# First stage of a streaming encoder step: squares of x moved off GpSimd, an accumulator read earlier, constants loaded later

## The chip, the cores and the metric

The kernel runs on one core of a Trainium2 chip. The time is the device time of one execution in microseconds. Engines are named as the profile names them: PE (TensorE, matmuls), PEld (its weight loads), DVE (VectorE), ACT (ScalarE), POOL (GpSimd) and SP (SyncE, which here only issues transfers). L196 is line 196 of the kernel before.

## The reference

One layer of a hybrid encoder over 256 prompt rows and 64 sample rows, 320 rows together, 2048 wide, all in float32. The stage that matters here is the first norm, the projection behind it, and the two gates:

```
def rmsnorm(x, g):
    y = xf * lax.rsqrt(jnp.mean(xf * xf, axis=-1, keepdims=True) + EPS)
    return (y * g)
...
    p = h @ w_in
    q, k, v, o, gates, u, z = jnp.split(p, SPLIT_IDX, axis=-1)
    gates = gates + b_gate
    ig = gates[..., :N_HEADS_M]
    lf = jax.nn.log_sigmoid(gates[..., N_HEADS_M:])
```

After it come a recurrence over four heads, a spatial gating over 128-row chunks (its weights are `wsp`, its bias `bsp`; `C0` is the carried state of the recurrence), an output projection of 2048 x 2048, and an MLP of 2048 x 8192 x 2048 with a squared ReLU.

## The kernel before

Activations lie transposed: 128 features on the partitions, the 320 rows (`NT`) along the free axis, so x is 16 tiles (`KT`) of 128 x 320. Float32 products are made of split operands: a value is rounded to `hi`, the rest is `lo`, and three matmuls (hi by hi, hi by lo, lo by hi) add up in PSUM. The norm's factor `R1` is a factor per row, so the projection runs on x times g, and R1 is multiplied in when an accumulator is read.

**First stage** (the loop over k, 16 tiles). For tile k, ACT makes `Xh` (L185) and the rounded weights `hi` of the 512 columns of k and the 100 gate columns (L193). DVE makes `Xl` (L194), `lo` (L196) and the low part of 36 gate columns, which it writes into `hi` (L197). POOL squares x (L204) and adds the square to `sacc` (L205). PE does 14 matmuls: four each at L208, L210 and L212 into four accumulators `kacc`, and two (L213, L214) into `gacc`. The raw weights of a tile, `w0raw`, lie in one of 4 buffers; SP issues the load of tile k+4 when tile k has been read. `hi` and `lo` have 5 buffers each.

**Behind it** stand 168 jobs of one form: 48 matmuls (L93, L94, L97) of 320 columns into one accumulator of tag `mm`, of which there are two. `gacc` holds one of these two. The first jobs are z0 to z7. A job's weights come in two halves of 512 KB into the same 4 raw buffers, and each half is split by ACT (L82) and DVE (L83) in program order. The raw buffer is free again when DVE's L83 has read it.

Each engine works in the order in which the program emits its instructions. `split_until(n)` emits the split of halves up to n, and, ahead of it, the loads four halves on. `gates()` is a generator: it sums `sacc` over the partitions with a matmul by ones (L292), makes `R1` (`rsqrt_to`, L120 to L123), and reads `gacc` by a copy on ACT (L295) and an add on DVE (L296); then it scales the four `kacc` and works out the gates, a piece at each call of `run_side()`. In the kernel before, four halves are split before the generator's first piece. `z_evac(c)` reads the accumulator of job z_c, with squares added to `sacc` on POOL; `zt` are the transposes of its result, which stand on PE ahead of the job two on.

`C0`, `wsp` and `bsp` are loaded from ACT's queue right after the first stage's code, and POOL masks `wsp` by four selects.

Of the kernel before, what the change touches and what calls it, by code (L numbers as in the profile page):

```python
# [19 lines left out]
AF = mybir.ActivationFunctionType  # L20
ALU = mybir.AluOpType
# [3 lines left out]
P = 128  # L25
D = 2048
# [3 lines left out]
NT = NP + NS  # L30
# [10 lines left out]
EPS = 1e-6  # L41
# [5 lines left out]
def emit(tc, A):  # L47
    nc = tc.nc
    act, dve, pe, pool, sp = nc.scalar, nc.vector, nc.tensor, nc.gpsimd, nc.sync
# [15 lines left out]
    def sdt(name):  # L65
        return ps.tile([P, 512], F32, tag="sd", name=name, bufs=6)
# [45 lines left out]
    R1 = cp.tile([P, NT], F32, name="R1")  # L112
    R2 = cp.tile([P, NT], F32, name="R2")
    sacc = cp.tile([P, NT], F32, name="sacc")
    sq_last = R2

    def rsqrt_to(out, ss, n, tmp, tag):

        r0, t = tmp(tag + "r"), tmp(tag + "t")
        act.activation(r0, ss, AF.Abs_reciprocal_sqrt, scale=1.0 / n)  # L120
        dve.tensor_tensor(t, r0, r0, ALU.mult)
        dve.scalar_tensor_tensor(t, ss, -0.5 / n, t, ALU.mult, ALU.mult)
        dve.scalar_tensor_tensor(out, t, 1.5, r0, ALU.add, ALU.mult)  # L123
# [4 lines left out]
    def tmp320(name, n=P):  # L128
        t = ap.tile([P, NT], F32, tag="t", name=name, bufs=5)
        return t[:n, :]  # L130
# [14 lines left out]
    def load_x(k0, k1):  # L145
        c = k0 // XC
        sp.dma_start(xraw[c][:, k0 - c * XC:k1 - c * XC, :], A["xg"][:, k0:k1, :])

    def load_w(k):
        w0raw[k] = wp.tile([P, W0], F32, tag="raw", name=f"w0raw{k}", bufs=4)  # L150
        for c0, c1 in W0A if k == 0 else ((0, W0),):
            sp.dma_start(w0raw[k][:, c0:c1], A["w0"][:, k, c0:c1])
# [17 lines left out]
    for c0, n in ((0, 256), (256, 128), (384, 64)):  # L170
        pool.affine_select(MASK[:, c0:c0 + n], MASK[:, c0:c0 + n], [[1, n]], ALU.is_ge, BIG,
                           base=0, channel_multiplier=-1)
# [3 lines left out]
    for k in range(KT):  # L176
        if k == 1:
            load_x(XC, 2 * XC)
        if k == XC:
            load_x(2 * XC, KT)  # L180
        if k + 4 < KT:
            load_w(k + 4)
        xr = xraw[k // XC][:, k % XC, :NT]
        gk = xraw[k // XC][:, k % XC, NT:]
        act.activation(Xh[k][:], xr, AF.Copy, scale=gk)  # L185
        w = w0raw[k]
        hi = wp.tile([P, W0], F32R, tag="hi", name=f"w0hi{k}")
        lo = wp.tile([P, 4 * P], F32R, tag="lo", name=f"w0lo{k}")
        if k == 0:
            for c0, c1 in W0A:  # L190
                dve.tensor_copy(hi[:, c0:c1], w[:, c0:c1])
        else:
            act.copy(hi[:], w[:])  # L193
        dve.scalar_tensor_tensor(Xl[k][:], xr, gk, Xh[k].bitcast(F32)[:], ALU.mult, ALU.subtract)  # L194
        hf = hi.bitcast(F32)
        dve.tensor_tensor(lo[:], w[:, :4 * P], hf[:, :4 * P], ALU.subtract)  # L196
        dve.tensor_tensor(hi[:, 4 * P + 64:], w[:, 4 * P:4 * P + 36], hf[:, 4 * P:4 * P + 36],  # L197
                          ALU.subtract)
        if k == 0:
            pool.tensor_tensor(sacc[:], xr, xr, ALU.mult)  # L200
            pool.tensor_scalar(sacc[:], sacc[:], D * EPS / P, None, ALU.add)
        else:
            sq = tmp320(f"sqx{k}")
            pool.tensor_tensor(sq, xr, xr, ALU.mult)  # L204
            pool.tensor_tensor(sacc[:], sacc[:], sq, ALU.add)  # L205
        first, last = k == 0, k == KT - 1
        for h in range(H):
            pe.matmul(kacc[h][:, :NT], hi[:, h * P:h * P + P], Xh[k][:], start=first, stop=False)  # L208
        for h in range(H):
            pe.matmul(kacc[h][:, :NT], hi[:, h * P:h * P + P], Xl[k][:], start=False, stop=False)  # L210
        for h in range(H):
            pe.matmul(kacc[h][:, :NT], lo[:, h * P:h * P + P], Xh[k][:], start=False, stop=last)  # L212
        pe.matmul(gacc[:100, :NT], hi[:, 4 * P:], Xh[k][:], start=first, stop=False)  # L213
        pe.matmul(gacc[:100, :NT], hi[:, 4 * P:], Xl[k][:], start=False, stop=last)  # L214


    C0 = ap.tile([P, H, VP], F32, name="C0")
    act.dma_start(C0[:], A["c0"])
    wsp = ap.tile([P, 4, P], F32, name="wsp")
    act.dma_start(wsp[:], A["wspT"])  # L220
    bsp = ap.tile([P, 4, P], F32, name="bsp")
    act.dma_start(bsp[:], A["bsp"].partition_broadcast(P))
    for g in range(4):
        pool.affine_select(wsp[:, g, :], wsp[:, g, :], [[1, P]], ALU.is_ge, 0.0,
                           base=0, channel_multiplier=-1)


    qT = [yslot("h", 8 + h, f"qT{h}") for h in range(H)]
# [34 lines left out]
    def later(gen, delay):  # L263
        coros.append([cur[0] + delay, gen])
# [19 lines left out]
    def row(i, name, n=4):  # L284
        return yslot("h" if i < 8 else "l", i % 8, name)[:n, :]
# [4 lines left out]
    def gates():  # L290
        s = sdt("ss1")
        pe.matmul(s[:, :NT], ones[:], sacc[:], start=True, stop=True)  # L292
        rsqrt_to(R1[:], s[:, :NT], D, tmp320, "r1")
        g36, glo = row(0, "g36", 36), row(1, "glo", 36)
        act.copy(glo, gacc[64:100, :NT])  # L295
        dve.tensor_tensor(g36, gacc[:36, :NT], glo, ALU.add)  # L296
        for h in range(H):
            dve.scalar_tensor_tensor(kT[h][:], kacc[h][:, :NT], float(P) ** -0.5, R1[:],
                                     ALU.mult, ALU.mult)
            if h == 1:  # L300
                yield
# [276 lines left out]
    pre = {}  # L578
# [100 lines left out]
    def load_to(n):  # L679
        while loaded[0] < min(n, len(halves)):  # L680
            j, h = halves[loaded[0]]
            j.load(h)
            loaded[0] += 1

    def split_until(n):
        while splitted[0] < min(n, len(halves)):
            load_to(splitted[0] + 4)
            j, h = halves[splitted[0]]
            j.split(h)
            splitted[0] += 1  # L690

    split_until(4)
    later(gates(), 0)
    for i, job in enumerate(jobs[:-1]):
        cur[0] = i
        if i == NA:
# [74 lines left out]
    k = 0  # L771
# [95 lines left out]
```

## Time and profile before

| | |
|---|---|
| median of 3 runs | 1364.63 us (1364.18 to 1366.63) |
| the profiled execution's own time | 1362.95 us |
| its span, first to last instruction | 1361.2 us |
| PE busy in the span | 1348.5 us, 99% |
| DVE, ACT, POOL busy | 688.3, 539.6, 55.4 us |
| moved by the DMA engines | 207.04 MB |

The span is 1.75 us shorter than the execution's time; what lies around it is not in the trace. Matmuls are pipelined and their ends are modelled, so a row of PE is read by the distance from start to start, and not by its duration. A row of DVE, ACT or POOL holds the time in which the instruction stood in the engine, so it can hold time in which it was held up; successive rows of one engine overlap by up to 0.1 us.

### The profile page before, as it was taken

Reading aid. Unit: us, or ns where it says so; the run is one execution under the profiler, and the core shown is the slowest. Engines: PE = TensorE matmul, PEld = TensorE weight load, DVE = VectorE, ACT = ScalarE, POOL = GpSimd, SP = SyncE. Lnnn points to the kernel's source line nnn. Section 1 sums busy time; section 2 is a strip of 40 time slices with the busy share of each in tenths; the row PEclk is TensorE's granted clock in tenths of the full one; section 3 lists DMA queues with packets and bytes.
Section 4 is the critical chain, followed back from the end, with each engine's and each line's share of the span. In section 5 each row is a group of like instructions: output and inputs, shape, how many; then the busy total and the mean of one; then the engine's idle time right before and its main releaser. Section 6 shows DMA issues by size and latency. Waiting matters only on the chain.

```text
span 1361.2 us, 22124 instructions
## 1 busy us (share of the span) xinstructions
PE 1348.5 (99%) x9197; PEld 1339.1 (98%) x9197; DVE 688.3 (51%) x967; ACT 539.6 (40%) x751; POOL 55.4 (4%) x89
## 2 busy tenths in 40 slices
PE   9999999999999999999999999999999999999997
PEld 8899999999999999999999999999999999999997
DVE  8785655565555544443344443444443444444444
ACT  5544465543444434333234433234433233444331
POOL 9410000000000000000000000000000000000000
PEclk9999999999999999999999999999999999999998
DMA  6745433434644444444444454444444444444432
GB/s 217 242 142 176 156 109 132 161 126 161 209 143 154 155 150 146 155 154 144 151 148 147 147 161 146 150 150 145 146 163 145 150 155 140 147 147 156 154 125 78
DMA packets 60023, 207.04 MB, mean 152 GB/s; under 512 B 6592, under 2 KB 9024, under 8 KB 59924
## 3 DMA queue, kind: packets, MB, share of 16 engines
q1 hardware_dynamic: 56932, 199.43, 45.1%
q10 hardware_dynamic: 2960, 6.17, 1.3%
q8 instruction: 72, 1.18, 0.3%
q14 instruction: 27, 0.22, 0.1%
q0 software_dynamic: 32, 0.03, 0.0%
HBM read 201.67 MB, written 3.94 MB: 151 GB/s over the span
## 4 chain that ended last, share of the span: by engine, by line
PE 95%; DVE 2%; issue 1%; DMA 1%; SPq 0%; ACT 0%; DVEq 0%; ACTq 0%
PE acc_f L93 22%; PE acc_f L94 22%; PE acc_f L97 22%; PE acc_out L93 3%; PE acc_out L97 3%; PE acc_out L94 3%; PE acc_u L93 1%; PE acc_v L97 1%; PE acc_o L97 1%; PE acc_v L93 1%; PE acc_o L93 1%; PE acc_u L97 1%; PE acc_o L94 1%; PE acc_v L94 1%; PE acc_u L94 1%; PE acc_z L93 1%
## 5 line engine op out<-in xcount | busy, mean ns | idle before, releaser
L83 DVE TENSOR_TENSOR lo_f<-raw_f,hi_f 128x1024 fp32r<-128x1024 f32 x256 | 306.2, 1222 | 139.2 <-ACT hi_f L82 137.3
L82 ACT CAST hi_f<-raw_f 128x1024 fp32r<-128x1024 f32 x256 | 261.9, 1052 | 236.4 <-PE acc_f L94 236.4
L93 PE MATMUL acc_f<-x2h,hi_f 128*128 128x320 f32 x1024 | 302.6, 309 | 0.0
L94 PE MATMUL acc_f<-x2l,hi_f 128*128 128x320 f32 x1024 | 302.4, 309 | 0.0
L94 PE MATMUL acc_f<-Yl,hi_f 128*128 128x320 f32 x1008 | 297.7, 309 | 0.0
L93 PE MATMUL acc_f<-Yh,hi_f 128*128 128x320 f32 x1008 | 297.6, 309 | 0.0
L93 PEld LDWEIGHTS acc_f<-x2h,hi_f 128*128 128x128 f32 x1024 | 192.3, 188 | 0.1
L94 PEld LDWEIGHTS acc_f<-x2l,hi_f 128*128 128x128 f32 x1024 | 192.3, 188 | 0.1
L93 PEld LDWEIGHTS acc_f<-Yh,hi_f 128*128 128x128 f32 x1008 | 189.3, 188 | 0.0
L94 PEld LDWEIGHTS acc_f<-Yl,hi_f 128*128 128x128 f32 x1008 | 189.3, 188 | 0.0
L97 PE MATMUL acc_f<-x2h,lo_f 128*128 128x320 f32 x1024 | 171.0, 309 | 0.0
L97 PE MATMUL acc_f<-Yh,lo_f 128*128 128x320 f32 x1008 | 168.3, 309 | 0.0
L97 PEld LDWEIGHTS acc_f<-x2h,lo_f 128*128 128x128 f32 x1024 | 155.4, 188 | 0.0
L97 PEld LDWEIGHTS acc_f<-Yh,lo_f 128*128 128x128 f32 x1008 | 153.0, 188 | 0.0
L653 ACT ACTIVATE f<-f 128x320 f32<-128x320 f32 x64 | 30.3, 473 | 262.3 <-DVE f L652 262.3
L659 DVE TENSOR_TENSOR xres<-acc_f,xres 128x320 f32<-128x320 f32 x63 | 31.0, 492 | 142.1 <-PE acc_f L97 142.1
L652 DVE SCALAR_TENSOR_TENSOR f<-acc_f,R 128x320 f32<-128x320 f32 x64 | 31.5, 492 | 136.8 <-PE acc_f L97 136.6
L94 PE MATMUL acc_out<-Yl,hi_out 128*128 128x320 f32 x256 | 75.6, 309 | 0.0
L93 PE MATMUL acc_out<-Yh,hi_out 128*128 128x320 f32 x256 | 75.6, 309 | 0.0
L280 DVE TENSOR_TENSOR Yl<-f,Yh 128x320 fp32r<-128x320 f32 x64 | 31.5, 493 | 66.1 <-ACT Yh L279 66.1
L93 PEld LDWEIGHTS acc_out<-Yh,hi_out 128*128 128x128 f32 x256 | 48.1, 188 | 0.0
L94 PEld LDWEIGHTS acc_out<-Yl,hi_out 128*128 128x128 f32 x256 | 48.0, 188 | 0.0
(333 smaller groups left out, 1667.8 us busy)
## 6 DMA issues: line engine op xcount, KB each, us to landing
raw_f<-w_ff SPq DMA_DIRECT2D x256, 512.0 KB, 3.9
raw_out<-w_out SPq DMA_DIRECT2D x32, 512.0 KB, 5.0
raw_z<-w_z SPq DMA_DIRECT2D x16, 512.0 KB, 5.0
raw_v<-w_v SPq DMA_DIRECT2D x16, 512.0 KB, 5.5
raw_o<-w_o SPq DMA_DIRECT2D x16, 512.0 KB, 5.0
raw_u<-w_u SPq DMA_DIRECT2D x16, 512.0 KB, 4.6
w0raw<-w SPq DMA_DIRECT2D x15, 306.0 KB, 2.9
raw_q<-w_q SPq DMA_DIRECT2D x8, 512.0 KB, 4.3
```

What stands on the lines that cost most here:

```text
L82: act.copy(hi[:], raw[:])
L83: dve.tensor_tensor(lo[:], raw[:], hi.bitcast(F32)[:], ALU.subtract)
L93: pe.matmul(o, self.hi[h][:, k, :], xh, start=(h == 0 and k == 0), stop=False)
L94: pe.matmul(o, self.hi[h][:, k, :], xl, start=False, stop=False)
L97: pe.matmul(o, self.lo[h][:, k, :], xh, start=False, stop=(h == 1 and k == 7))
L280: dve.tensor_tensor(l_[:], src, h_.bitcast(F32)[:], ALU.subtract)
L652: dve.scalar_tensor_tensor(t[:], acc, 0.0, R2[:], ALU.max, ALU.mult)
L653: act.activation(t[:], t[:], AF.Square)
L659: dve.tensor_tensor(xres[m], acc, xres[m], ALU.add)
```

## The change

The squares of x are made on ACT. The first goes straight into `sacc`, and DVE adds the 15 others, the constant included with the first of these. POOL has no arithmetic left in this stage. `gates()` reads `gacc` before it makes `R1`, and yields once after `R1`; the caller emits this first piece after one split half and not after four. `C0`, `wsp` and `bsp` are loaded, and `wsp` is masked, in `load_late()`, which is called ahead of the matmuls of job 3 (z3).

```
         if k == 0:
-            pool.tensor_tensor(sacc[:], xr, xr, ALU.mult)
-            pool.tensor_scalar(sacc[:], sacc[:], D * EPS / P, None, ALU.add)
+            act.activation(sacc[:], xr, AF.Square)
         else:
             sq = tmp320(f"sqx{k}")
-            pool.tensor_tensor(sq, xr, xr, ALU.mult)
-            pool.tensor_tensor(sacc[:], sacc[:], sq, ALU.add)
+            act.activation(sq, xr, AF.Square)
+            if k == 1:
+                dve.scalar_tensor_tensor(sacc[:], sq, D * EPS / P, sacc[:], ALU.add, ALU.add)
+            else:
+                dve.tensor_tensor(sacc[:], sacc[:], sq, ALU.add)
...
+    def load_late():
+        act.dma_start(C0[:], A["c0"])
+        act.dma_start(wsp[:], A["wspT"])
+        act.dma_start(bsp[:], A["bsp"].partition_broadcast(P))
+        for g in range(4):
+            pool.affine_select(wsp[:, g, :], wsp[:, g, :], [[1, P]], ALU.is_ge, 0.0,
+                               base=0, channel_multiplier=-1)
...
         pe.matmul(s[:, :NT], ones[:], sacc[:], start=True, stop=True)
-        rsqrt_to(R1[:], s[:, :NT], D, tmp320, "r1")
         g36, glo = row(0, "g36", 36), row(1, "glo", 36)
         act.copy(glo, gacc[64:100, :NT])
         dve.tensor_tensor(g36, gacc[:36, :NT], glo, ALU.add)
+        rsqrt_to(R1[:], s[:, :NT], D, tmp320, "r1")
+        yield
...
+    pre[3] = load_late
+    split_until(1)
+    gate_chain = gates()
+    next(gate_chain)
     split_until(4)
-    later(gates(), 0)
+    later(gate_chain, 0)
```

DVE at the end of the first stage, before: the last two tiles (xl, lo, the 36 columns), four halves of jobs z0 and z1, the three operations of R1, and the read of the gate accumulator, g.

```order
L194 SCALAR_TENSOR_TENSOR xl_117<-xraw_121,xh_101 128x320
L196 TENSOR_TENSOR w0lo_528<-w0raw_426,w0hi_527 128x512
L197 TENSOR_TENSOR w0hi_527<-w0raw_426,w0hi_527 128x36
L194 SCALAR_TENSOR_TENSOR xl_118<-xraw_121,xh_102 128x320
L196 TENSOR_TENSOR w0lo_552<-w0raw_452,w0hi_551 128x512
L197 TENSOR_TENSOR w0hi_551<-w0raw_452,w0hi_551 128x36
L83 TENSOR_TENSOR lo_z_0_637<-raw_z_0_628,hi_z_0_636 128x1024
L83 TENSOR_TENSOR lo_z_1_643<-raw_z_1_630,hi_z_1_642 128x1024
L83 TENSOR_TENSOR lo_z_0_649<-raw_z_0_632,hi_z_0_648 128x1024
L83 TENSOR_TENSOR lo_z_1_655<-raw_z_1_634,hi_z_1_654 128x1024
L121 TENSOR_TENSOR r1t<-r1r 128x320
L296 TENSOR_TENSOR g_666<-gacc,glo 36x320
...
```

The same place of DVE after the change (its lines have other numbers: the read of `gacc` is L300, the added sums are L207).

```order
L194 SCALAR_TENSOR_TENSOR xl_118<-xraw_121,xh_102 128x320
L196 TENSOR_TENSOR w0lo_551<-w0raw_451,w0hi_550 128x512
L197 TENSOR_TENSOR w0hi_550<-w0raw_451,w0hi_550 128x36
L207 TENSOR_TENSOR sacc<-sacc,sqx_556 128x320
L83 TENSOR_TENSOR lo_z_0_629<-raw_z_0_620,hi_z_0_628 128x1024
L300 TENSOR_TENSOR g_634<-gacc,glo 36x320
L121 TENSOR_TENSOR r1t<-r1r 128x320
L122 SCALAR_TENSOR_TENSOR r1t<-ss_632,r1t 128x320
L123 SCALAR_TENSOR_TENSOR R_81<-r1t,r1r 128x320
L83 TENSOR_TENSOR lo_z_1_647<-raw_z_1_622,hi_z_1_646 128x1024
L83 TENSOR_TENSOR lo_z_0_653<-raw_z_0_624,hi_z_0_652 128x1024
L83 TENSOR_TENSOR lo_z_1_659<-raw_z_1_626,hi_z_1_658 128x1024
```

Each tile has one instruction more on DVE, and the read of `gacc` and the three operations of R1 have moved past three of the four halves.

ACT at the same place, before: the three loads of the constants stand between the last tile and z0.

```order
L185 ACTIVATE xh_102<-xraw_121 128x320
L193 CAST w0hi_551<-w0raw_452 128x612
L218 DMA C_574<-c 128x1032
L220 DMA wsp<-wspT 128x512
L222 DMA bsp<-bsp 128x512
L82 CAST hi_z_0_636<-raw_z_0_628 128x1024
L82 CAST hi_z_1_642<-raw_z_1_630 128x1024
L82 CAST hi_z_0_648<-raw_z_0_632 128x1024
L82 CAST hi_z_1_654<-raw_z_1_634 128x1024
L120 ACTIVATE r1r<-ss_658 128x320
L295 COPY glo<-gacc 36x320
```

And after.

```order
L185 ACTIVATE xh_102<-xraw_121 128x320
L193 CAST w0hi_550<-w0raw_451 128x612
L203 ACTIVATE sqx_556<-xraw_121 128x320
L82 CAST hi_z_0_628<-raw_z_0_620 128x1024
L299 COPY glo<-gacc 36x320
L120 ACTIVATE r1r<-ss_632 128x320
L82 CAST hi_z_1_646<-raw_z_1_622 128x1024
L82 CAST hi_z_0_652<-raw_z_0_624 128x1024
L82 CAST hi_z_1_658<-raw_z_1_626 128x1024
```

No table load was added on ACT, the copy of `gacc` now stands behind one half, and the three loads are gone from here.

POOL after the change, further on: the masks of `wsp` stand between two of the z jobs' additions to `sacc` (before, they stood ahead of all of them).

```order
L394 TENSOR_SCALAR sacc<-sacc 128x320
L397 TENSOR_TENSOR sacc<-sacc,zr_796 128x320
L407 MEMSET z2g 64x1024
L397 TENSOR_TENSOR sacc<-sacc,zr_879 128x320
L228 AFFINE_SELECT wsp<-wsp 128x128
L228 AFFINE_SELECT wsp<-wsp 128x128 x3
L397 TENSOR_TENSOR sacc<-sacc,zr_966 128x320
```

The first of them waits for the load of `wsp`, and the addition for z3 stands behind it. The order of PE's matmuls and of SP's loads is what it was.

## Rows read from the trace of the kernel before

**Rows 1.** Waits of PE, whole span: us in total, times, longest.
```profile
PE acc_z L93 <- DVE g L296: 1.7, 1, 1.7
PE ssf_s L737 <- ACT R L732: 0.7, 1, 0.7
```

**Rows 2.** Waits of PEld, whole span, the two longest.
```profile
PEld kacc L212 <- DVE w0lo L196: 4.6, 15, 0.3
PEld acc_z L93 <- DVE g L296: 2.0, 1, 2.0
```

**Rows 3.** Timeline, DVE, one tile: start, us, line, operation.
```profile
34.30 1.37 DVE L196 TENSOR_TENSOR w0lo<-w0raw,w0hi 128x512 fp32r<-128x512 f32 x1
35.59 0.71 DVE L197 TENSOR_TENSOR w0hi<-w0raw,w0hi 128x36 fp32r<-128x36 f32 x1
36.22 0.54 DVE L194 SCALAR_TENSOR_TENSOR xl<-xraw,xh 128x320 fp32r<-128x320 f32 x1
36.68 1.37 DVE L196 TENSOR_TENSOR w0lo<-w0raw,w0hi 128x512 fp32r<-128x512 f32 x1
```

**Rows 4.** Timeline, POOL, the same tile.
```profile
33.94 1.18 POOL L205 TENSOR_TENSOR sacc<-sacc,sqx 128x320 f32<-128x320 f32 x1
35.08 1.17 POOL L204 TENSOR_TENSOR sqx<-xraw 128x320 f32<-128x320 f32 x1
```

**Rows 5.** Busy time, tile 1 to 15: PE, PEld, DVE, ACT, POOL; clock, DMA share, GB/s.
```profile
9.50:42.87 33.37, 32.76 (x196) 28.52 (x196) 33.37 (x44) 16.05 (x27) 31.67 (x28) 1.00 0.65 206
```

**Rows 6.** Timeline, DVE, first tile and last tile.
```profile
6.38 0.68 DVE L196 TENSOR_TENSOR w0lo<-w0raw,w0hi 128x512 fp32r<-128x512 f32 x1
...
42.74 0.18 DVE L197 TENSOR_TENSOR w0hi<-w0raw,w0hi 128x36 fp32r<-128x36 f32 x1
```

**Rows 7.** Groups by line and shape, DVE and ACT: busy us, mean ns.
```profile
L83 DVE TENSOR_TENSOR lo_z<-raw_z,hi_z 128x1024 fp32r<-128x1024 f32 x16 | 19.0, 1214 | 7.8 <-ACT hi_z L82 7.8
...
L628 DVE TENSOR_TENSOR sacc<-sacc,sq 128x320 f32<-128x320 f32 x27 | 13.2, 489 | 7.0 <-ACT sq L624 7.0
...
L624 ACT ACTIVATE sq<-xres 128x320 f32<-128x320 f32 x29 | 13.5, 464 | 59.0 <-DVE xres L659 59.0
L193 ACT CAST w0hi<-w0raw 128x612 fp32r<-128x612 f32 x15 | 10.6, 707 | 13.3 <-PE gacc L214 5.6 <-DMA w0raw<-w 5.5 <-DVE w0lo L196 2.0
...
L185 ACT ACTIVATE xh<-xraw 128x320 fp32r<-128x320 f32 x16 | 9.0, 560 | 3.7 <-DMA xraw<-xg 3.7
```

**Rows 8.** The chain that ended last, two runs of eight matmuls.
```profile
92.74 1.17 PE acc_z L97 x8
...
96.26 1.17 PE acc_z L97 x8
```

**Rows 9.** Page, DMA issues: KB each, us to landing.
```profile
w0raw<-w SPq DMA_DIRECT2D x15, 306.0 KB, 2.9
```

**Rows 10.** Busy time from 40 to 50 us; the last column is GB/s.
```profile
40.00:50.00 10.00, 9.91 (x65) 9.19 (x64) 6.33 (x8) 4.08 (x4) 6.40 (x22) 1.00 0.86 316
```

**Rows 11.** Timeline, PE: tile 1's first matmuls, and the sum of squares behind tile 15.
```profile
8.12 0.75 PE L208 MATMUL kacc<-xh,w0hi 128*128 128x320 f32 x4
...
43.85 0.70 PE L292 MATMUL ss<-sacc,ones 128*128 128x320 f32 x2
```

**Rows 12.** Timeline, PE, from job z0 to job z1.
```profile
50.26 1.34 PE L97 MATMUL acc_z<-xh,lo_z 128*128 128x320 f32 x8
...
53.56 0.30 PE L94 MATMUL acc_z<-xl,hi_z 128*128 128x320 f32 x1
```

**Rows 13.** The z weights' tile view, its line on transfers.
```profile
DMA to landing us min/median/max: 3.7/5.0/6.6
```

**Rows 14.** DMA issues up to 70 us: the largest constant.
```profile
C<-c ACTq DMA_DIRECT2D x1, 516.0 KB, 5.5
```

**Rows 15.** Timeline, ACT: the casts of job z5's two halves.
```profile
70.31 1.98 ACT L82 CAST hi_z<-raw_z 128x1024 fp32r<-128x1024 f32 x2
```

**Rows 16.** The chain that ended last: PE's transposes ahead of z5.
```profile
82.70 0.33 PE zt L405 x3
```

More of the change, by code (lines that the diff above doesn't have):

```diff
@@ L217, in emit @@
     C0 = ap.tile([P, H, VP], F32, name="C0")
-    act.dma_start(C0[:], A["c0"])
     wsp = ap.tile([P, 4, P], F32, name="wsp")
-    act.dma_start(wsp[:], A["wspT"])
     bsp = ap.tile([P, 4, P], F32, name="bsp")
[L222 to L225, printed above, removed]
+    def load_late():
[5 more added lines that the diff above has]
+                               base=0, channel_multiplier=-1)
     qT = [yslot("h", 8 + h, f"qT{h}") for h in range(H)]
```

## The prediction

> **What bounds the kernel now.** I begin with what PE waits for, since PE fills the span. After the start it waits twice: 1.7 us at the first matmul of job z1, for DVE's read of the gate accumulator, and 0.7 us at the very end [rows 1]. So from z1 on the time is a row of matmuls without a hole, and only what happens before that can change the end. PE's weight loads tell a second thing: in the first stage they wait 15 times, once in each tile from the second on, always for DVE's `lo` [rows 2]. PE looks busy there (32.76 of 33.37 us) because the ends of matmuls are modelled, but DVE is busy for all 33.37 us and POOL for 31.67 [rows 5]. The tile's period is DVE's: from one `lo` to the next, 36.68 - 34.30 = 2.38 us [rows 3].
>
> What fills that period: `lo` for 1.37 us, the 36 gate columns for 0.71, `xl` for 0.54, laid end to end with a small overlap [rows 3]. Two of these are not DVE's own work. The `lo` of the first tile, same shape, took 0.68 us, and the 36 columns of the last tile, when POOL had finished, took 0.18 [rows 6]. In the tile shown, `lo` begins while POOL's sum is running and ends 0.55 us after that sum ends at 33.94 + 1.18 = 35.12; the 36 columns end at 36.30, POOL's square at 36.25 [rows 3, 4]. The two engines hold each other up in turn. The row thus says that of 2.38 us some 1.2 are waiting.
>
> The Trainium skill ("SBUF — State Buffer", Who interferes with whom) has a rule for this: a VectorE instruction with two SBUF inputs and a GpSimd instruction that reads SBUF exclude each other, and the later one waits for the other to end. These rows agree in `lo` and in the 36 columns; `xl`, which has two SBUF inputs as well, stayed at 0.54, so its turn came when POOL was the one to wait. By the rule alone, as by the rows, the waits go when POOL's reads go.
>
> **The squares.** Per tile DVE loses the waits and gains one addition. With durations without POOL: `lo` 0.68, 36 columns 0.18 [rows 6], `xl` 0.54 [rows 3], the sum 0.49, taken from the same addition of the later norms [rows 7]. That makes 1.89 us, or about 1.6 from start to start with the overlaps. ACT has 0.56 + 0.71, and gets a square at 0.46 from the same later norms [rows 7]: 1.73. These stand against PE's own 14 matmuls. A matmul of 320 columns takes (96.26 - 92.74) / 24 = 0.1467 us in the jobs [rows 8], so a tile takes 2.05 us: more than DVE's or ACT's sum even without overlap. So I take PE as the next bound of this stage. The clock was 1.00 of full speed there, which is the 2.4 GHz level [rows 5], and there is nothing above it.
>
> The weights have to keep up. A raw buffer comes back for tile k+4 when tile k has been read; load 2.9 us [rows 9], cast 0.71, `lo` 0.68, 36 columns 0.18 make about 4.5 us for four tiles, 1.1 us each, and even a load twice as long leaves 1.85. The transfers move 206 GB/s in this stage [rows 5]; at 2.05 instead of 2.38 us a tile they need 240, and 316 has been reached in 40 to 50 us [rows 10].
>
> Tile 1's first matmul starts at 8.12 us [rows 11], after a first tile whose few waits are for its own loads, so I leave that start where it is. Fifteen tiles of 14 matmuls then take 30.81 us, and the sum of squares behind them starts at 38.93 instead of 43.85 [rows 11]: **4.92 us earlier**. Bounds: if nothing is gained, 0; if tile 1's start also moved as far forward as its `lo` wait of 0.3 us [rows 2], 5.2.
>
> **The gate accumulator.** z0's last eight matmuls start at 50.26 and advance 1.17 us [rows 12, 8], so the second matmul of z1 could start at 51.58; it starts at 53.56 [rows 12]. That is 1.98 us, the 2.0 us which the weight load waits [rows 2]. After the change the copy and the add stand behind one half only. `gacc` is complete at about 39 us, so it is read by about 40, while z0 occupies PE until 38.93 + 0.30 + 48 x 0.1467 = 46.27. The wait is gone with 6 us to spare: **1.98 us**. What now comes later is the split of z0's second half and of z1: copy, add and the three operations of R1 put it at about 41.5 us on DVE. PE wants z0's second `lo` at 39.23 + 40 x 0.1467 = 45.1, and it is done at 42.7; z1's two halves follow at 43.9 and 45.1, wanted at 48.6 and 52.1. A step further: z2's second half is loaded only when z0's second `lo` has freed its buffer at 42.7. With the median landing of 5.0 us [rows 13], a cast of about 1.0 [rows 15] and a `lo` of 1.21 [rows 7], z0's accumulator is read at 50.6; PE comes to z2 at 53.3. With the slowest landing, 6.6 us, it is 52.2, still in time. I charge nothing, and up to 1 us in the range.
>
> **The constants.** Their loads took about 1 MB (the largest is 516 KB [rows 14]) beside the first loads of z. Nothing in PE waited for those, so taking them away gives nothing. At the new place, ACT issues them after z2's evacuation and before the casts of z5. Those casts stood at 70.31 us and PE came to z5 at 82.70 [rows 15, 16]: a lead of 12 us, against 1.4 us of issuing. In bytes, 1 MB at 316 GB/s [rows 10] is 3.3 us of all transfers, which the lead covers as well. POOL waits for `wsp` there with z3's addition behind it; the sum of these additions is wanted five jobs later. I charge 0, and 3.3 us as the price if the cover fails. POOL's memsets move to the first microseconds, where POOL had its first square; 0 too.
>
> **Sum.** 4.92 + 1.98 = 6.90. The profiled execution took 1362.95 us, so 1356.05 by its own scale, with a span of about 1354.3. That execution was 1.68 us quicker than the median; against the median of 1364.63 the forecast is **1357.7 us**.
>
> **Rivals.**
> 1. DVE stays the bound, and the added sum lengthens it: *slower*. For it speaks that DVE shows no idle time at all in this stage [rows 5], and the change adds work to it. If `lo` and the 36 columns kept their length for another reason than POOL, the period would be 2.38 + 0.49 = 2.87 us, 14 periods 6.9 us longer, less 1.98: 1369.5. It turns slower in total above a period of 2.38 + 1.98 / 14 = 2.52 us. Against it stand the 0.68 and the 0.18 [rows 6]. The Trainium skill ("Perfetto Trace Analysis", Optimizing Scalar/DVE Operations) would give work of a saturated DVE to ScalarE or even GpSimd, which is against these 15 additions; it says in the same place that GpSimd shares a port with DVE, and the rows side with that. Chance 0.04.
> 2. The stage speeds up less: loads, or semaphores between ACT and DVE, hold the tile at about 2.2 us. ACT waited 5.5 us in all for the weights [rows 7]. Then 15 x 0.15 = 2.2 us are lost: 1359.9. Chance 0.08.
> 3. The constants at the fourth job hold up weights: 3.3 us back, 1361.0. The 12 us of lead speak against it. Chance 0.03.
> 4. Only the accumulator's wait goes, because another engine takes over at the old period: 1362.7, no measurable change. Chance 0.03.
>
> **How the numbers follow.** The forecast itself gets 0.82, with 1356.2 to 1359.0 as its own range (1 us of a new wait, and the spread of the runs shown, which is about 1 us to either side). The range 1355.6 to 1360.9 takes in rival 2 and most of rival 3. A change of 0.2%, 2.7 us, is about what can be told from none, so 1361.9 and below counts as faster: the forecast, rivals 2 and 3 make 0.93; rival 4 and a little of the others 0.04 as the same; rival 1 0.03 to 0.04 as slower. I give 0.92, 0.04, 0.04.
>
> **What would show it.** In the profile after: `lo` at about 0.68 us and the 36 columns at 0.2 in every tile; DVE with idle time between tiles; no 0.3 us waits of weight loads for `lo`; the sum-of-squares matmul at about 39 us; no wait of z1 for the gate add; DVE's added sums at 0.49 and ACT's squares at 0.46; the rest of PE without a hole, and the span near 1354.3. Wrong would be: `lo` still above 1 us, ACT waiting for weights in each tile, or a new wait of PE at z2 or between z4 and z6.

## The result and the profile after

The changed kernel took **1358.07 us** (median of 4 runs, 1356.24 to 1358.90), the kernel before beside it 1364.57. The ratio is 0.9948, with a 95% interval of 0.9930 to 0.9965: 6.5 us faster by the medians, 7.1 by the ratio. The profiled execution took 1358.22 us, with a span of 1356.5 us.

PE's waits in the profile after, whole span, to be read beside [rows 1]:

```profile
PE warm L164 <- DVE eps L110: 1.1, 1, 1.1
PE ssf_s L747 <- ACT R L742: 0.6, 1, 0.6
PE kacc L210 <- ACT w0hi L193: 0.5, 1, 0.5
PE kacc L210 <- DVE w0hi L191: 0.2, 1, 0.2
```

The wait of z1 for the gate add is gone. What is left lies in the first 8.3 us and at the very end. One tile on DVE (L207 is the added sum), the counterpart of [rows 3], and the stretch that answers to [rows 5]:

```profile
11.41 0.68 DVE L196 TENSOR_TENSOR w0lo<-w0raw,w0hi 128x512 fp32r<-128x512 f32 x1
12.01 0.19 DVE L197 TENSOR_TENSOR w0hi<-w0raw,w0hi 128x36 fp32r<-128x36 f32 x1
12.12 0.48 DVE L207 TENSOR_TENSOR sacc<-sacc,sqx 128x320 f32<-128x320 f32 x1
12.52 0.55 DVE L194 SCALAR_TENSOR_TENSOR xl<-xraw,xh 128x320 fp32r<-128x320 f32 x1
12.98 0.68 DVE L196 TENSOR_TENSOR w0lo<-w0raw,w0hi 128x512 fp32r<-128x512 f32 x1
```

```profile
10.43:39.18 28.75, 28.75 (x198) 28.75 (x197) 22.45 (x56) 19.31 (x40) 0.00 (x0) 1.00 0.80 266
```

`lo` has fallen from 1.37 to 0.68 us and the 36 columns from 0.71 to 0.19. With one instruction more, DVE needs 12.98 - 11.41 = 1.57 us for a tile and stands idle for 6.3 us of the 28.75. PE's weight loads (the third number) now fill the stretch, where they had been busy for 28.52 of 33.37. PE's timeline, with the places of [rows 11] and [rows 12] (the start of tile 1, the sum of squares, the last matmuls of z0, the second matmul of z1):

```profile
8.28 0.85 PE L210 MATMUL kacc<-xh,w0hi 128*128 128x320 f32 x4 [0.48 <-ACT w0hi L193]
...
39.18 0.70 PE L297 MATMUL ss<-sacc,ones 128*128 128x320 f32 x2
...
45.58 1.34 PE L97 MATMUL acc_z<-xh,lo_z 128*128 128x320 f32 x8
...
46.90 0.31 PE L94 MATMUL acc_z<-xl,hi_z 128*128 128x320 f32 x1
```

The sum of squares starts at 39.18 and not at 43.85, z1's second matmul at 46.90 and not at 53.56: a lead of 6.66 us, against 6.90 forecast. Yet the spans differ by 1361.2 - 1356.5 = 4.7 us only. The other 1.9 us go at the end. These are the last matmuls, 64 columns each, and the sum behind them, first after the change, then before it:

```profile
1341.82 1.06 PE L734 MATMUL acc_s<-Yh,lo_f 128*128 128x64 f32 x8
1342.71 1.47 PE L734 MATMUL acc_s<-Yh,hi_f 128*128 128x64 f32 x8
1343.99 1.89 PE L734 MATMUL acc_s<-Yl,hi_f 128*128 128x64 f32 x8
...
1348.19 0.69 PE L747 MATMUL ssf_s<-R,ones 128*128 128x64 f32 x2 [0.60 <-ACT R L742]
```

```profile
1349.36 1.06 PE L724 MATMUL acc_s<-Yh,hi_f 128*128 128x64 f32 x8
...
1352.90 0.69 PE L737 MATMUL ssf_s<-R,ones 128*128 128x64 f32 x2 [0.70 <-ACT R L732]
```

Up to 1342.71 the changed kernel is 6.65 us ahead. From there to the last sum it takes 5.48 us, where the kernel before took 3.54. The busy times by stretch, after the change, show why (the granted clock stands third from the end):

```profile
1342.50:1343.00 0.50, 0.50 (x7) 0.50 (x6) 0.47 (x2) 0.00 (x0) 0.00 (x0) 1.00 0.00 0
1343.00:1343.50 0.50, 0.50 (x5) 0.50 (x5) 0.47 (x2) 0.00 (x0) 0.00 (x0) 0.70 0.00 0
1343.50:1344.00 0.50, 0.50 (x5) 0.50 (x4) 0.50 (x2) 0.00 (x0) 0.00 (x0) 0.50 0.00 0
```

The clock falls to its lower level, 1.2 GHz, in the middle of the narrow matmuls. In the profile before it fell too, but only when they were over. The profile of e3 below, which has the end of the kernel before, shows the same fall in the middle of them:

```profile
1349.00:1350.00 1.00, 1.00 (x6) 1.00 (x6) 0.97 (x4) 0.00 (x0) 0.00 (x0) 0.50 0.00 0
```

So this is no wait that the change has made. It is a loss that falls on some executions and not on others, of either kernel: the four runs of the changed kernel were 1358.22, 1358.90 and 1357.91 us with a mean clock of 0.995, and 1356.24 us with 0.997.

### The profile page after: what moved, and what is told of

Read it like the earlier page. It is cut to its first block, busy times and chain, and to the rows that moved or that the text cites. A ratio compares the mean times of both kernels' runs of the same rounds, so it can differ in the third digit from the quotient of the medians.

```text
span 1356.5 us, 22119 instructions
## 1 busy us (share of the span) xinstructions
PE 1346.4 (99%) x9197; PEld 1341.5 (99%) x9197; DVE 676.4 (50%) x982; ACT 542.2 (40%) x767; POOL 18.3 (1%) x57
## 4 chain that ended last, share of the span: by engine, by line
PE 99%; DMA 0%; DVE 0%; SPq 0%; ACT 0%; issue 0%; DVEq 0%
PE acc_f L94 22%; PE acc_f L93 22%; PE acc_f L97 22%; PE acc_out L93 3%; PE acc_out L97 3%; PE acc_out L94 3%; PE acc_u L93 1%; PE acc_z L97 1%; PE acc_v L97 1%; PE acc_o L97 1%; PE acc_v L93 1%; PE acc_o L94 1%; PE acc_z L93 1%; PE acc_u L97 1%; PE acc_v L94 1%; PE acc_o L93 1%
```

## The experiments

Theory A is that of the prediction: POOL's reads held DVE, the early read of `gacc` removes the wait of z1, the constants' place is worth nothing, and the parts add up. Theory B is that the wait of z1 was a consequence of the slow stage, and the parts overlap.

### One part at a time

**e1_squares**: the kernel before with the first hunk of the diff alone.

> The kernel before with only the squares of x moved to ACT and DVE; gate accumulator and constants as before. Theory A (the parts add up, as in the prediction's sum): the sum of squares starts at about 39.2 us, z1 still waits about 2 us for the gate add, so 4.7 us faster than before. Theory B (the gate wait was itself caused by late landings of the z weights, which are asked for when first-stage buffers come free): with a faster first stage the landings come earlier too, the wait of z1 shrinks below 0.5 us, so 6 to 6.7 us faster than before. If POOL was not what held DVE up, the stage keeps its length and the time is that of before or up to 7 us more.

Measured: 1357.41 us (5 runs, 1356.04 to 1359.64) against 1364.29, ratio 0.9955 (0.9943 to 0.9968): 6.9 us faster by the medians, 6.1 by the ratio, where the whole change had 6.5 and 7.1: no difference can be told. The profile says the same more sharply. In the profiled execution the clock stayed up to the last matmuls, as in that of the kernel before, and the spans are 1354.2 and 1361.2 us: 7.0 less. The sum of squares starts at 38.79. The gate add, and z0's last matmuls on PE:

```profile
45.17 0.47 DVE L298 TENSOR_TENSOR g<-gacc,glo 36x320 f32<-36x320 f32 x1
...
45.19 1.34 PE L97 MATMUL acc_z<-xh,lo_z 128*128 128x320 f32 x8
```

The add still stands behind four split halves and R1, and is done at 45.64, before z1 is due at 46.36. No wait is left. Theory B.

**e2_gate**: the kernel before with the hunk in `gates()` and the order at the call.

> The kernel before with only the order around the gates changed (one split, then the read of the gate accumulator, then R1, then three splits). First stage as before, sum of squares at 43.85 us. Theory A and B: the 2.0 us wait of z1 is gone, 2.0 us faster than before. Rival: another wait takes its place at z1 (its weights land late beside the constants' loads): less than 1 us faster.

Measured: 1362.26 us (11 runs), ratio 0.9987 (0.9979 to 0.9996): 2.0 us faster by the medians, 1.8 by the ratio (0.5 to 2.9), and z1's wait for the gate add is gone from the profile. The sum of squares is at 44.69 there and not at 43.85 as told: in the first two tiles POOL's reads met other instructions of DVE than in the profile before (the first `lo` took 1.20 us in place of 0.68, an `xl` 1.05 in place of 0.54). Alone, the early read does what the prediction says.

**e3_late**: the kernel before with `load_late()` at job 3.

> The kernel before with only the three constants' loads and the masks moved to job 3. Theory A (constants cost nothing before): no change, gate wait of z1 still 2 us. Theory B (their 1 MB delays the z halves, ACT's casts of four halves, and behind these the copy of the gate accumulator): z1's wait falls from 2.0 to below 0.5 us, 1.5 to 2 us faster than before.

Measured: 1363.03 us (11 runs), 1.3 us less than before, ratio 0.9995 (0.9986 to 1.0004): the interval holds no change as well. The profile tells more. ACT's cast ahead of R1 and z1's first matmul:

```profile
48.15 1.05 ACT L82 CAST hi_z<-raw_z 128x1024 fp32r<-128x1024 f32 x1 [0.90 <-DMA raw_z<-w_z]
...
52.36 0.41 PE L93 MATMUL acc_z<-xh,hi_z 128*128 128x320 f32 x1 [0.57 <-DVE g L298]
```

The fourth half is cast at 48.15 and not at 49.09, the gate add starts at 51.83 and not at 52.78, and z1's wait on PE is 0.57 us, not 1.7. Of these 1.15 us, 0.2 are not the add's: PE came later, with the sum of squares at 44.05. So the constants did delay the z weights and, behind them, the gate add. Theory A's zero for them is wrong in this kernel; by the clock of the runs alone it stays open.

The three parts measured alone make 6.9 + 2.0 + 1.3 = 10.2 us by the medians, together 6.5 (8.6 and 7.1 by the ratios): two of them remove a wait that the first removes as well. The traces show it without the scatter of the runs. From the sum of squares to the second matmul of z1 it is 9.71 us in the kernel before, 7.72 in e1, 7.90 in e2, 8.56 in e3, and 7.72 with all three.

### What POOL did to DVE

**e5_pool_reads** and **e6_pool_writes**: the changed kernel with work on POOL whose result (in R2, overwritten later) nothing uses. The second has `pool.memset(R2[:], 0.0)` twice in place of the two lines.

```diff
+        pool.tensor_tensor(R2[:], xr, xr, ALU.mult)
+        pool.tensor_tensor(R2[:], xr, xr, ALU.mult)
         first, last = k == 0, k == KT - 1
```

> The changed kernel with two multiplications of x by itself on POOL in each tile of the first stage, into a buffer that nothing reads (the work that POOL had, without its results). Theory A (DVE and POOL exclude each other when both read two operands from SBUF): lo goes back above 1 us and the 36 columns above 0.5, the tile's period to 2.4 to 2.8 us, and the time is 5 to 11 us more than that of the changed kernel: 1363 to 1369. Rival (moving the sums' dependence off POOL was what counted, POOL's mere activity costs nothing): 1358, period 2.05.

> The changed kernel with two memsets of 128 x 320 on POOL in each tile of the first stage, into a buffer that nothing reads before it is overwritten. Theory A (it is reads that exclude each other): period 2.05, lo 0.68, time of the changed kernel, 1358. Rival (any SBUF traffic of POOL holds DVE up): lo and the 36 columns longer; whether the time moves depends on whether DVE's tile passes 2.05 us.

Measured: with the reads 1366.03 us (10 runs), 2.4 more than the kernel before beside it (1363.61); with the writes 1357.68 (4 runs). DVE with POOL reading, one tile:

```profile
22.96 1.01 DVE L194 SCALAR_TENSOR_TENSOR xl<-xraw,xh 128x320 fp32r<-128x320 f32 x1
23.89 1.20 DVE L196 TENSOR_TENSOR w0lo<-w0raw,w0hi 128x512 fp32r<-128x512 f32 x1
25.01 0.71 DVE L197 TENSOR_TENSOR w0hi<-w0raw,w0hi 128x36 fp32r<-128x36 f32 x1
...
26.05 1.00 DVE L194 SCALAR_TENSOR_TENSOR xl<-xraw,xh 128x320 fp32r<-128x320 f32 x1
```

The period is 3.09 us, longer than the 2.8 expected at most, since now `xl` is held up too (1.01 in place of 0.54), which before was the one that went first. The time is in the range told all the same, because POOL runs ahead and has done its last read before DVE has done its tiles. DVE and then POOL, at that point:

```profile
36.25 1.20 DVE L196 TENSOR_TENSOR w0lo<-w0raw,w0hi 128x512 fp32r<-128x512 f32 x1
...
38.87 0.68 DVE L196 TENSOR_TENSOR w0lo<-w0raw,w0hi 128x512 fp32r<-128x512 f32 x1
...
40.44 0.68 DVE L196 TENSOR_TENSOR w0lo<-w0raw,w0hi 128x512 fp32r<-128x512 f32 x1
...
36.98 1.05 POOL L209 TENSOR_TENSOR R<-xraw 128x320 f32<-128x320 f32 x1
```

POOL's last read ends at 38.03. The next `lo` is back at 0.68 us and the period at 40.44 - 38.87 = 1.57, within one execution, while POOL goes on with memsets up to 40.6 us. With POOL writing, DVE and then POOL:

```profile
12.58 0.68 DVE L196 TENSOR_TENSOR w0lo<-w0raw,w0hi 128x512 fp32r<-128x512 f32 x1
13.18 0.19 DVE L197 TENSOR_TENSOR w0hi<-w0raw,w0hi 128x36 fp32r<-128x36 f32 x1
...
12.57 0.37 POOL L208 MEMSET R<- 128x320 f32 x1
13.00 0.36 POOL L209 MEMSET R<- 128x320 f32 x1
```

The memsets ran ahead, one after the other up to 17.6 us, some five tiles of DVE; beside them DVE's durations are those without POOL. The Trainium skill ("SBUF — State Buffer", Who interferes with whom) says just this: a VectorE instruction with two SBUF inputs contends with a GpSimd instruction that reads SBUF, and not with one that only writes it. Both runs agree. With e1, which takes POOL's reads away, and e5, which puts them back, the cause of the stage's old period is shown.

### How near DVE is to being the bound

**e7_dve_squares**: the changed kernel with

```diff
-            act.activation(sq, xr, AF.Square)
+            dve.tensor_tensor(sq, xr, xr, ALU.mult)
```

> The changed kernel with the 15 later squares on DVE as well, none on ACT. DVE then has five operations a tile. If durations add up: 0.54 + 0.69 + 0.19 + 0.49 + 0.49 = 2.40 us a tile, DVE the bound, 15 x 0.35 = 5 us slower than the changed kernel: 1363. If what counts is start to start (1.57 us a tile seen in the changed kernel, plus 0.41): 1.98 us, just under PE's 2.05, and the time stays within 0.5 us of 1358.

Measured: 1359.40 us (4 runs, 1356.91 to 1359.72), against 1357.68 of e6 on the same chip (1357.54 to 1359.67). Neither number was met for DVE's tile:

```profile
23.25 0.19 DVE L197 TENSOR_TENSOR w0hi<-w0raw,w0hi 128x36 fp32r<-128x36 f32 x1
23.35 0.49 DVE L203 TENSOR_TENSOR sqx<-xraw 128x320 f32<-128x320 f32 x1
23.87 0.49 DVE L207 TENSOR_TENSOR sacc<-sacc,sqx 128x320 f32<-128x320 f32 x1
...
25.35 0.19 DVE L197 TENSOR_TENSOR w0hi<-w0raw,w0hi 128x36 fp32r<-128x36 f32 x1
```

The period is 25.35 - 23.25 = 2.10 us, just above PE's 2.05. Independent instructions overlap by 0.06 to 0.1 us; the sum, which reads the square just made, starts 0.52 us after it and has no overlap. Durations added (2.40) say too much, starts of independent ones (1.98) too little.

Yet DVE did not hold PE up here. PE's rows at the start of tile 1 and at the sum of squares:

```profile
9.53 0.92 PE L210 MATMUL kacc<-xh,w0hi 128*128 128x320 f32 x4
...
40.51 0.70 PE L297 MATMUL ss<-sacc,ones 128*128 128x320 f32 x2
```

That is 30.98 us, against 39.18 - 8.28 = 30.90 in the changed kernel: DVE was ahead when tile 1 began, and 15 times 0.05 us did not use that up. What this execution lost, it lost before: tile 1 starts 1.25 us later than in the changed kernel, because the matmuls of the first tile went at half the pace (see e10 below).

### The clock at the end

**e4_tail192**, **e8_tail128**: the changed kernel with wider last matmuls. With w = 192 or 128, the last w columns are multiplied, and only the last 64 results are used:

```diff
-        c, n = parts[p]
+        c, n = parts[p] if p == 0 else (slice(NT - w, NT), w)
...
-        dve.tensor_tensor(xl[:, c], acc[p][:, :n], xl[:, c], ALU.add)
+        a0 = 0 if p == 0 else w - NS
+        dve.tensor_tensor(xl[:, c], acc[p][:, a0:a0 + n], xl[:, c], ALU.add)
```

> The changed kernel with its last 48 matmuls 192 columns wide and not 64 (the last 64 columns are used, the other 128 are computed a second time and thrown away). Theory A (the 1.9 us missing between the gain at z1 and the gain at the end is TensorE's clock falling to half during the narrow matmuls): the clock stays at its upper level until these matmuls are over in every run, mean clock 0.997, the pass takes 5.3 us as in the profile of before, all runs near 1356.2 us. Rival (the clock falls there whatever the matmuls' width): runs at 1358 as often as before, mean clock 0.995. If wider matmuls cost PE time of their own, the pass is longer by up to 48 x 0.03 = 1.4 us.

> The changed kernel with its last 48 matmuls 128 columns wide (64 of them thrown away). Same theories as for 192: if more columns per matmul keep the clock up and 128 suffice, all runs near 1356.2 us with a mean clock of 0.997; if 128 are too few, some runs at 1358 with 0.995; if width has nothing to do with it, runs as in the changed kernel.

Measured: 1355.85 us with 192 columns (5 runs, 1355.58 to 1356.05) and 1355.76 with 128 (4 runs, 1355.55 to 1355.95): all runs together, none near 1358. The wider matmuls, here 192, cost nothing:

```profile
1342.45 1.06 PE L734 MATMUL acc_s<-Yh,hi_f 128*128 128x192 f32 x8
1343.35 1.05 PE L734 MATMUL acc_s<-Yl,hi_f 128*128 128x192 f32 x8
...
1345.93 0.43 PE L748 MATMUL ssf_s<-R,ones 128*128 128x64 f32 x2 [0.64 <-ACT R L743]
```

Eight matmuls advance 0.89 us whether 64, 128 or 192 columns wide. That the clock stayed up with the wider ones is shown by the 9 runs (mean clock 0.997 to 0.999); why it did is not shown here.

**e9_before_tail**, **e10_squares_tail**, **e11_after_tail**: the same edit with 128 columns on the kernel before, on e1 and on the whole change (the kernel of e8 again), on one chip.

> The kernel before with its last 48 matmuls 128 columns wide (64 of them thrown away). If the kernel before, too, loses 1.9 us in those of its executions in which the clock falls during the narrow matmuls, all runs lie together at 1362.3 to 1363.0 us, where the quicker half of its own runs lies, instead of spreading up to 1365. If that loss belongs to the changed kernel alone, the times are those of before.

> The kernel before with the squares moved and the 128 wide tail. Theory B (with a faster first stage the gate accumulator is read in time anyway): 1355.7, the same as the whole change with that tail. Theory A (the parts add up): 1357.7, since the early read is missing.

> The whole change with the 128 wide tail again, on the same chip as the two others. 1355.8 within 0.3 us, as the first time; the distance to the kernel before with the same tail is then the change's worth without the clock: 6.7 us if the distances in the profiles hold (6.66 us at z1's second matmul).

Measured: 1363.02 us (11 runs, 1362.22 to 1364.91), 1356.60 (5 runs, 1355.99 to 1357.87) and 1355.68 (5 runs, 1355.59 to 1356.35). The last, as e8, is the fastest version of the study: ratio 0.9934 (0.9920 to 0.9947) against the kernel before beside it. On the kernel before, the wider end alone changes nothing that can be told: ratio 0.9996 (0.9987 to 1.0004).

The first two did not come out as told: their runs still lie in two groups. Both profiles are of longer executions, and show two more places where the clock is low. In e9 it falls behind the gate wait:

```profile
53.52 0.41 PE L93 MATMUL acc_z<-xh,hi_z 128*128 128x320 f32 x1 [1.84 <-DVE g L296]
...
54.55 0.47 PE L94 MATMUL acc_z<-xl,hi_z 128*128 128x320 f32 x1
54.82 0.47 PE L93 MATMUL acc_z<-xh,hi_z 128*128 128x320 f32 x1
...
55.00:56.00 1.00, 1.00 (x6) 1.00 (x5) 1.00 (x2) 0.00 (x0) 0.00 (x0) 0.50 0.57 234
```

Matmuls follow each other at 0.267 us and not at 0.147, from 54.06 to 57.5, which is some 1.5 us lost; the clock is 0.50. In e10 it is at the start of the program. Its first matmuls, then those of the kernel before:

```profile
4.55 0.88 PE L210 MATMUL kacc<-xh,w0hi 128*128 128x320 f32 x2
...
6.85 1.27 PE L212 MATMUL kacc<-xl,w0hi 128*128 128x320 f32 x4
```

```profile
4.55 0.55 PE L208 MATMUL kacc<-xh,w0hi 128*128 128x320 f32 x2
...
6.51 0.85 PE L210 MATMUL kacc<-xl,w0hi 128*128 128x320 f32 x4
```

Four matmuls advance 1.06 us in e10 in place of 0.59, the pace of the lower clock level, and the two at 4.55, ahead of any wait for weights, are slow already. So the clock has not fallen here; it has not yet risen. The kernel before starts at the lower pace as well, as its warm-up (16 matmuls on `ones`) shows beside the first stage, by their weight loads (3.5 us in all, 330 ns for one, against 189):

```profile
L164 PEld LDWEIGHTS warm<-ones 128*128 128x128 f32 x16 | 3.5, 330 | 1.1 <-DVE eps L110 1.1
L208 PEld LDWEIGHTS kacc<-xh,w0hi 128*128 128x128 f32 x64 | 10.1, 189 | 1.2 <-DVE w0hi L191 1.2
```

The column of the granted clock reads 1.00 in all of these stretches; the trace's own list of clock levels begins only where the pace rises, at 10.7 us in e10 and at 4.6 in the kernel before. In seven of the 13 profiles it is at 4.3 to 6.3 us, in six (e2, e3, e5, e7, e9, e10) at 9.7 to 10.7; why is not shown. In e10 it costs about 2 us, with the sum of squares at 40.86 against 38.79 in e1. In e9 it costs nothing, with the sum at 43.91 against 43.85 in the kernel before: there DVE, and not PE, sets the pace of the stage.

Taking the quickest runs, 1362.22, 1355.99 and 1355.59, the whole change is worth 6.6 us (7.3 by the medians of e9 and e11), the squares alone 6.2. Whether the other two parts still give the last 0.4 us is not settled by five runs each. The profiles in which the clock rose early and stayed up speak against it: their spans are 1354.2 us with the squares alone (e1), and 1354.0, 1354.2 and 1354.1 with the whole change (e4, e8, e11).

## Why the prediction was right, step by step

**DVE's waits, and PE as the next bound: right.** `lo` 0.68, the 36 columns 0.19, sum 0.48, square 0.47 were within 0.02 us of the rows they were taken from. PE's pace is 0.1467 us a matmul from 10.43 to 39.18 us (196 matmuls). The term of 4.92 us measured 4.67: tile 1 started at 8.28, 0.16 us later than assumed, since its cast waited for its weights, and the 15 tiles took 30.90 us, not 30.81. "I leave that start where it is" was the step that slipped; in the other profiles with an early rise of the clock that start lies between 7.95 and 8.15.

**The gate accumulator: the size right, the reason only half.** z1 gained 6.66 - 4.67 = 1.99 us, forecast 1.98. But the term was put down to the early read, and e1 shows that the squares alone remove it. The sum came out because it counted that wait once, whichever part removes it. The prediction worked out when the add would come in the new order, and never in the old order with the faster stage. There the buffers of the z weights come free sooner, their landings, four casts and the add behind them all move forward, and the add makes it by 0.7 us.

**The constants: wrong as a statement on the kernel before, harmless in the sum.** "Nothing in PE waited for those" took the last link of a chain for the whole of it: PE waited for the gate add, the add stood behind ACT's casts, and the four casts ahead of it waited 8.3 us in all for z weights that landed beside the constants, 7.2 without them. e3 brings the add 0.95 us forward. At the new place they cost nothing, as forecast: PE has no wait there.

**The rest of PE without a hole: wrong by 1.9 us in the profile.** The span was forecast at 1354.3 and was 1356.5; the run with the mean clock of 0.997 had 1354.5. Nothing in the prediction knew of the clock. Since the kernel before has such runs too, and its median with them, the forecast against the median (1357.7) came close to 1358.07; that much of the closeness is luck.

**The rivals.** DVE staying the bound is refuted by 1.57 us a tile, 6.3 us of idle time, and e5 and e6. The loads did make ACT wait (4.0 us in all), but with DVE and ACT tiles ahead of PE none of it reached PE after 8.3 us. The late constants held up nothing.

## What to carry to other kernels

An engine that reads 100% busy may be waiting inside its instructions: compare the duration of the same shape at a moment when the suspected partner is idle, before adding up its load. When two edits aim at waits that follow each other, ask of each wait whether it would still be there after the other edit alone; measured alone, these three parts summed to 10.2 us and gave 6.5. And where runs of one kernel lie in two groups, look for the stretch where the clock was low, at the very start too and by the pace of the matmuls, before explaining a difference of that size.

## What the runs showed of the hardware beyond what was expected

Matmuls with 128 x 128 weights advance at 0.1117 us whether 64, 128 or 192 columns wide. At 64 columns the clock fell in some executions and cost 1.9 us; at 128 and 192 it did not in 14 runs of the changed kernel. The clock also fell in one profile (e9) behind PE's wait of 1.84 us at 53 us, and cost some 1.5 us; in the kernel before's own profile it stayed up behind a wait of 1.72. So a short wait of PE can cost nearly as much again as it lasts, and the gate wait of the kernel before carried this risk with it. The program starts at the pace of the lower clock, and the rise came as early as 4.3 us in one execution (e1) and as late as 10.7 in another (e10), which was worth 2 us where PE was the bound; where DVE was (e9), the late rise cost nothing.

A read by POOL holds up a DVE instruction with two inputs in SBUF: 128x512 went from 0.68 to 1.20 us in e5, and back to 0.68 in the same execution as soon as POOL's reads were over.
